# Layer A's first pass: the key and value products of a unit's two tiles in one PSUM bank ahead of both query products

## The chip, the cores and the metric

The kernel runs as one program on 1 core of one Trainium2 chip. The metric is the device time of one execution in microseconds (us), taken as the median of several runs. The core has five engines that run side by side and meet only at semaphores: PE (TensorE, matrix products, with PEld for its weight loads), ACT (ScalarE), DVE (VectorE), POOL (GpSimd) and SP (SyncE, which here only issues DMA transfers). PE writes its results to PSUM, eight banks of 128 partitions by 512 fp32 numbers; ACT and DVE read them from there.

## The reference

An inference step of a streaming encoder with two attention layers, over a prompt of 2048 tokens and a sample of 64 tokens with cached keys and values. Cut to what matters here:

```
def project(x, norm_g, w_in, q_g, k_g, n_heads, n_kv):
    h = rms_norm(x, norm_g)
    p = h @ w_in                          # (tokens, 1024) @ (1024, width)
    q, k, v, gate = jnp.split(p, ...)
    q = rms_norm(q per head, q_g)
    k = rms_norm(k per head, k_g)
    return q, k, v, gate

def gated_attention_layer(...):
    qp, kp, vp, gp = project(x_p, ...)
    op = prompt_band_attention(qp, kp, vp, past_chunks, bias_fn, sinks)
    y_p = x_p + (op * silu(gp)) @ w_out
    ...                                   # the same for the sample, with its cache
```

Layer A (the first) has 16 query heads of 64 and 2 key and value heads, a window of the own and two past chunks of 64 frames, a bias by relative position and a sink per head. Layer B has 16 key and value heads and a window of the own and eight past chunks. Everything is fp32 outside; inside, each product is made of three: high part by high part, high by low and low by high.

## The kernel before

**Tiles and units.** Tokens are worked in tiles of 128. Two tiles make a unit of 256 tokens (`units`, u = 0 to 7); the 64 sample tokens are a ninth unit (u == NU) with a single tile. The list `order` puts the sample in front of the last unit: 0, 1, 2, 3, 4, 5, 6, sample, 7.

**Passes.** Layer A goes over all units four times, `qd` = 0 to 3. Each pass projects 256 columns of queries and 256 of gates for four heads: a *query product* of 512 columns by 8 blocks of the model dimension by 3 matmuls, 24 matmuls of 512 columns (in `project`, L796, L797, L798; the sample's are L791 and L792, 16 of them). The first pass, `qd` = 0, also projects the 128 key and 128 value columns: a *key/value product* of 24 matmuls of 256 columns. Later passes reuse keys and values.

**PSUM.** Tag "pj" has two banks for the products, "o" one for attention outputs and small sums, "tp" one for transposes, and a pool "pa" with tag "sa" has four score banks. A buffer is given to a product when PE comes to its first matmul, from those that are free by the planner's own forecast of the times; the work on PE keeps the order in which the code emits it, and the other engines' instructions are ordered by the planner.

**Who empties a "pj" bank.** A key/value product is read by one ACT copy (`evacuate`, L819). A query product is read by ACT twice (`evacuate_a`: squares L835, gates L836) and last by DVE, which scales the queries by their norms (`norm_ps`, L890) after a sum on DVE (L883) and two steps on POOL (L886, L887). `in_banks(1)`, called before each new "pj" bank, emits the norms of all banks but the newest.

**The order around the change.** `layer_a` has a list of items, one per tile and pass. `Filler` is the stream of projection matmuls; `gen` of a unit yields after each block. `pipeline` walks the items: step i emits the scores of item i, then lets the filler run to 0.3 of the step, emits the transposes of probabilities of item i-1 (`values`), runs the filler to 0.6, emits the key transposes of item i+2 (`keys`, first pass only), runs to 0.8, emits the query and gate transposes (`turned`), runs to 0.95, emits the products with the values of item i-1 (`outputs`, L1452), and runs the filler to the end of the step. The end is the `mark` of item i+3, the point of the filler at which that item's products are finished.

In the first pass `gen` emits, for a unit's tiles 0 and 1: key/value product of 0, query product of 0, key/value product of 1, query product of 1, each in a "pj" bank of its own. Only the unit that comes last in `order` (u = 7, `heads_up`) emits both key/value products first, in two banks. Unit 0 has an order of its own (`first`) that the change does not touch. In unit 1 the scale of the values (`value_scales`, L290 to L297) is set with a small matmul into the "tp" bank, the token scales are made after tile 0's key/value product (`token_scales`), and rows of later units are loaded and squared (`row_scales`, L772) after each tile's.

Of the kernel before, what the change touches and what calls it, by code (L numbers as in the profile page):

```python
# [24 lines left out]
NU = SEQ // UT  # L25
# [33 lines left out]
def hybrid_encoder_kernel(  # L59
# [47 lines left out]
    def psum(tag, cols, bufs, pool=None):  # L107
        uid[0] += 1
        return (pool or pp).tile([P, cols], F32, tag=tag, name=f"{tag}_{uid[0]}", bufs=bufs)

    scores_pool = [None]
    psum_a = psum_b = lambda tag, cols, bufs: psum(tag, cols, bufs, scores_pool[0])
# [23 lines left out]
    held = {}  # L136
# [65 lines left out]
    def tp_bank():  # L202
        run_all("scales")
        return psum("tp", 512, 1)
# [85 lines left out]
        everywhere(9, row[:, 56:59])  # L290

    def value_scales():
        ps = tp_bank()
        nc.tensor.matmul(
            ps[:, 0:2], ones[0:1, 0:1].to_broadcast([1, P]), row[:, 44:46], start=True, stop=True
        )
        nc.vector.tensor_copy(sva, ps[:, 0:2])  # L297
# [427 lines left out]
    def token_scales(unit, x, ps):  # L725
        for q, q2 in zip(x.items, x.squares):
            bg.run(q)
            bg.run(q2)
        part = x.sum[0]
        _, T, tiles = unit  # L730
        sums_to_scales(0, tiles[0][0], [part[:, i * P : (i + 1) * P] for i in range(len(tiles))], ps)
# [49 lines left out]
    def project(tile_, xc, w, C, res, ps=None):  # L781
        tt, t0, n = tile_
        if ps is None:
            in_banks(1)
            ps = psum("pj", 512, 2)
            held["pj"].append([])
        for k in range(KC):
            wh, wl = weights_of(w, k)
            xh, xl = xc.parts[k // 2]
            if xl is None:  # L790
                nc.tensor.matmul(ps[:, :C], xh[:, k % 2, :], wh, start=k == 0, stop=False)  # L791
                nc.tensor.matmul(ps[:, :C], xh[:, k % 2, :], wl, start=False, stop=k == KC - 1)  # L792
                cost = 2 * C / 2400
            else:
                xh, xl = (a[:, k % 2, t0 : t0 + n] for a in (xh, xl))
                nc.tensor.matmul(ps[:n, :C], xh, wh, start=k == 0, stop=False)  # L796
                nc.tensor.matmul(ps[:n, :C], xh, wl, start=False, stop=False)  # L797
                nc.tensor.matmul(ps[:n, :C], xl, wh, start=False, stop=k == KC - 1)  # L798
                cost = 3 * C / 2400
            if k < KC - 1:  # L800
                yield cost
        res.append(ps)
        return cost
# [98 lines left out]
    def in_banks(n):  # L902
        while len(held["pj"]) > n:
            for it in held["pj"].pop(0):
                bg.run(it)
# [219 lines left out]
    def layer_a():  # L1125
        items = []
# [3 lines left out]
        def add_unit(qd, place, unit):  # L1130
            u, T, tiles = unit
            mine = []
            for tl in tiles:
                it = Item()
                it.qd, it.unit, it.tile, it.ready, it.todo = qd, unit, tl, False, []
                mine.append(it)
            items.extend(mine)

# [22 lines left out]
            def take_kv(it, ps):  # L1161
                tt, t0, n = it.tile
                last = u == NU
                it.kv = pr = evacuate(0, tt, n, ps, 256, 0)
                kn, v = pr[:n, 0:128], pr[:n, 128:256]
                if last:
                    split_v(n, v, VS[:, 1])
                else:
                    held["v"].append((VT[:, tt], v.rearrange("p (h d) -> p h d", d=HD)))
                if u == 1 and it is mine[0]:  # L1170
                    value_scales()
                while u and held["v"]:
                    vt, vv = held["v"].pop(0)
                    split_to(vt[:, :, 0:HD], vt[:, :, HD:P], vv, sva[:, 0:1])
                it.knorm = head_norm(n, kn, False)
                if last:
                    it.knorm.append(store_kv(0, slice(0, n), kn, v, ka_s[64:128, :], va_s[64:128, :]))
                elif tt == NT - 1:
                    it.knorm.append(store_kv(0, slice(0, n), kn, v, ka_p, va_p))
# [45 lines left out]

            def gen():
                xc = st.x.pop((qd, u))
                heads_up = qd == 0 and unit is order[-1]
                if heads_up:
                    for it in mine:  # L1230
                        out = []
                        c = yield from project(it.tile, xc, st.wkv, 256, out)
                        take_kv(it, out[0])
                        yield c
                for it in mine:
                    if qd == 0 and not heads_up:
                        out = []
                        c = yield from project(it.tile, xc, st.wkv, 256, out)
                        if u == 1 and it is mine[0]:
                            token_scales(unit, xc, psum("o", 512, 1))  # L1240
                        take_kv(it, out[0])
                        if u == 1:
                            row_scales(order[it.tile[0]])
                        yield c
                    out = []
                    c = yield from project(it.tile, xc, st.w[qd], 512, out)
                    take_qg(it, out[0])
                    if place:
                        spread_step()
                    if it is mine[-1]:  # L1250
                        if qd == 2 and place == 0:
                            bias_vectors_b()
                            keep(1)
                            held["heads"] += [(1, h) for h in range(16)]
                    yield c

            for it in mine:
                filler.total += 8 * (2 if it.tile[2] < P else 3) * (512 if qd else 768) / 2400
                it.mark = filler.total
            if qd == 0 and u == 0:  # L1260
                mine[0].mark = filler.total
            if qd == 0 and unit is order[-1]:
                mine[0].mark += 8 * 3 * 256 / 2400
            filler.add(prefetch, weights if place == 0 else None, first if qd == 0 and u == 0 else gen, 3 * (qd > 1))

        for qd in range(4):
# [1 line left out]
                add_unit(qd, place, unit)  # L1268

        def keys(it):  # L1270
            for q in it.knorm:
                bg.run(q)
            tt, t0, n = it.tile
            tp = psum_a("sa", 512, 4)[:, :n]
            transpose(tp, it.kv[:n, 0:128])
            gk = (kf, ksc)[it.unit[0] == NU][:, 0:1]
            if it.unit[0] == NU:
                kd = [a[:, CA : CA + TS] for a in (KSA, KSB)]
            else:
                kd = [a[:, tt * P : (tt + 1) * P] for a in (KA, KB)]  # L1280
            for kk, rows in zip(kd, halves):
                nc.scalar.activation(kk[0:64], tp[rows], AF.Identity, scale=gk[rows])
            for kk, rows in zip(kd, halves):
                nc.vector.scalar_tensor_tensor(
                    kk[64:128], tp[rows], gk[rows], wide(kk[0:64]),
                    op0=ALU.mult, op1=ALU.subtract,
                )
# [220 lines left out]
        def pipeline():  # L1508
            N = len(items)
            for i in range(-3, N + 1):  # L1510
                c0 = filler.done
                end = c0 + 5.2
                if i + 3 < N:
                    end = max(items[i + 3].mark, c0 + AVG_A)
                filler.attending = i >= 0
                scales_ahead(i)
                if 0 <= i < N:
                    scores(items[i])
                    if i == N - 1:
                        held["scored"] = True  # L1520
                    bg.share(AL, AP_, 3)
                filler.to(c0 + 0.3 * (end - c0))
                if 0 <= i < N:
                    turn_a(items[i])
                if 0 <= i - 1:
                    values(items[i - 1])
                    bg.share(AL, AP_, 3)
                if 0 <= i + 2 < N and items[i + 2].qd == 0:
                    filler.to(c0 + 0.6 * (end - c0))
                    keys(items[i + 2])  # L1530
                filler.to(c0 + 0.8 * (end - c0))
                turned(items[i + 2] if 0 <= i + 2 < N else None, items[i - 1] if 0 <= i - 1 else None)
                filler.to(c0 + 0.95 * (end - c0))
                if 0 <= i - 1:
                    outputs(items[i - 1])
                filler.to(end)
                assert i + 3 >= N or items[i + 3].ready
# [1083 lines left out]
```

## Time and profile before

| what | before |
|---|---|
| median of 3 runs | 2065.02 us (2062.98 to 2066.77) |
| the profiled execution's own time | 2071.44 us |
| its span, first to last instruction | 2069.7 us |
| mean granted TensorE clock | 0.992 |
| ACT busy | 1438.7 us (70%) |
| DVE busy | 1440.7 us (70%) |
| POOL busy | 1134.8 us (55%) |

A profile is one execution. Busy time is the time in which an engine has an instruction running. A line such as L796 is the line of the kernel that made the instruction, and "out<-in" names the tiles that it writes and reads. "idle before <-X" says which instruction ended the engine's idle time. The first pass of layer A, with the start-up, fills about the first 220 us of the span; all later passes and layer B have no key/value product of this kind.

### The profile page before, as it was taken

The numbers are of one execution on the slowest core, as the hardware profiler recorded it, in microseconds if no ns is written. First come the engines' busy times: TensorE is split into PE (matmuls) and PEld (weight loads), VectorE is DVE, ScalarE is ACT, GpSimd is POOL, SyncE is SP. The second block draws the span as 40 slices with busy tenths as digits, with TensorE's granted clock in tenths as the row PEclk, the third lists the DMA queues.
The fourth block names the chain that finished last, engine by engine and source line by source line (L and its number), as shares of the span: only waits on it lengthen the run. The fifth ranks groups of instructions, "written<-read, shape, count | busy, mean of one in ns | idle before, by whom it ended". The sixth has DMA issues, their size and how long they took to land.

```text
span 2069.7 us, 40501 instructions
## 1 busy us (share of the span) xinstructions
PE 1975.7 (95%) x12723; PEld 1382.1 (67%) x12723; DVE 1440.7 (70%) x4163; ACT 1438.7 (70%) x3560; POOL 1134.8 (55%) x1529
## 2 busy tenths in 40 slices
PE   7899999999999999989999999999999999999999
PEld 6777777777877888545555555555555555557788
DVE  7666877877778433677667676676767767677673
ACT  6887888777789443377677787786877778687330
POOL 5665565544446323477556575665656656565540
PEclk9999999999999999999999999999999999999999
DMA  8878887998776555698989788897997978698753
GB/s 264 260 210 233 230 215 207 238 243 243 206 187 192 168 177 162 229 235 219 237 177 237 177 201 220 168 253 162 212 211 182 215 167 187 151 189 205 189 158 106
DMA packets 593816, 420.20 MB, mean 203 GB/s; under 512 B 403696, under 2 KB 522880, under 8 KB 593568
## 3 DMA queue, kind: packets, MB, share of 16 engines
q1 hardware_dynamic: 593600, 417.60, 79.9%
q8 instruction: 101, 1.65, 0.3%
q14 instruction: 115, 0.94, 0.1%
HBM read 248.68 MB, written 73.43 MB: 156 GB/s over the span
## 4 chain that ended last, share of the span: by engine, by line
PE 58%; DVE 12%; DMA 10%; ACT 8%; issue 6%; POOL 5%; SPq 1%; POOLq 0%; ACTq 0%; DVEq 0%
PE pj L796 11%; PE pj L798 10%; PE pj L797 10%; PE o L1908 4%; DMA pt<-values 3%; PE sb L1744 2%; PE pj L2164 2%; PE sb L1745 2%; PE pj L2166 2%; PE pj L2165 2%; PE tp L1054 2%; PE pj L2413 2%; PE pj L2417 2%; PE pj L2416 2%; DVE p L1748 1%
## 5 line engine op out<-in xcount | busy, mean ns | idle before, releaser
L796 PE MATMUL pj<-wh,xx 128*128 128x512 f16 (+2 forms) x1648 | 642.9, 390 | 19.8 <-ACT pa L819 9.1
L798 PE MATMUL pj<-wh,xx 128*128 128x512 f16 (+2 forms) x1648 | 624.6, 379 | 0.0
L1801 POOL TENSOR_TENSOR values<-p,values 128x640 f16<-128x640 f32 (+4 forms) x256 | 328.2, 1282 | 206.9 <-ACT values L1800 202.7
L797 PE MATMUL pj<-wh,xx 128*128 128x512 f16 x1024 | 389.9, 381 | 1.3 <-DVE wh L582 1.3
L1760 ACT ACTIVATE p<-p,nm 128x640 f32<-128x640 f32 (+5 forms) x264 | 199.6, 756 | 181.4 <-DVE nm L1753 148.7
L1748 DVE CUSTOM_DVE_ANT_0 p<-sb,BT 128x640 f32<-128x640 f32 (+5 forms) x272 | 196.4, 722 | 148.1 <-PE sb L1745 120.9
L797 PE MATMUL pj<-wl,xx 128*128 128x512 f32 (+1 forms) x624 | 234.8, 376 | 2.3 <-DVE wl L582 2.3
L887 POOL TENSOR_TENSOR f<-f,mhalf 128x4 f32<-128x4 f32 x182 | 188.0, 1033 | 11.7
L798 PEld LDWEIGHTS <-xx 128*128 128x128 f16 x1024 | 100.6, 98 | 123.6 <-issue 3.8
L1561 POOL TENSOR_TENSOR o<-gt,o 128x256 f32<-128x256 f32 (+1 forms) x132 | 106.4, 806 | 139.5 <-ACT p L1391 63.9
L1800 ACT CAST values<-p 128x640 f16<-128x640 f32 (+4 forms) x256 | 168.2, 657 | 12.7 <-DMA pt<-values 6.5
L1391 ACT ACTIVATE p<-p,nm 128x257 f32<-128x257 f32 (+2 forms) x272 | 134.3, 496 | 59.3 <-DVE nm L1380 26.6
L797 PEld LDWEIGHTS <-xx 128*128 128x128 f16 x1024 | 100.6, 98 | 84.2 <-issue 4.9
L796 PEld LDWEIGHTS <-xx 128*128 128x128 f16 x1024 | 100.6, 98 | 82.0 <-issue 1.9
L1908 PEld LDWEIGHTS <-values 128*128 128x128 f16 x1344 | 123.8, 98 | 41.2 <-issue 2.8
L1908 PE MATMUL o<-pt,values 128*128 128x256 f16 (+1 forms) x1344 | 144.7, 256 | 3.6 <-DMA pt<-values 3.6
L796 PEld LDWEIGHTS pj<-wh,xx 128*128 128x128 f32 x624 | 118.6, 190 | 40.3 <-ACT pa L819 11.0
L798 PEld LDWEIGHTS pj<-wh,xx 128*128 128x128 f32 x624 | 118.4, 190 | 23.1
L886 POOL TENSOR_TENSOR f<-f,small 128x4 f32<-128x4 f32 x182 | 38.5, 211 | 172.5 <-DVE f L883 152.7
L797 PEld LDWEIGHTS pj<-wl,xx 128*128 128x128 f32 x624 | 119.1, 191 | 17.6 <-DVE wl L582 3.2
L1556 ACT COPY o<-o 64x256 f32<-64x256 f32 (+1 forms) x264 | 96.1, 364 | 37.8 <-PE o L1908 27.3
L678 POOL TENSOR_TENSOR xx<-xraw,xx 128x512 fp32r<-128x512 f32 (+3 forms) x80 | 97.4, 1233 | 44.3 <-ACT xx L677 44.0
(389 smaller groups left out, 5157.7 us busy)
## 6 DMA issues: line engine op xcount, KB each, us to landing
xx<-xsb SPq DMA_DIRECT2D x112, 512.0 KB, 4.3
xx<-xsa SPq DMA_DIRECT2D x88, 512.0 KB, 5.0
xsa<-xx SPq DMA_DIRECT2D x32, 512.0 KB, 4.2
wl<-in_w_in_b_dram SPq DMA_DIRECT2D x64, 256.0 KB, 4.8
wraw<-in_w_in_b_dram SPq DMA_DIRECT2D x56, 256.0 KB, 3.6
xraw<-in_x_dram SPq DMA_DIRECT2D x40, 256.0 KB, 4.4
xraw<-oga SPq DMA_DIRECT2D x32, 264.0 KB, 3.2
xraw<-ogb SPq DMA_DIRECT2D x32, 264.0 KB, 3.5
```

Of the source, the lines that this page charges most:

```text
L678: nc.gpsimd.tensor_tensor(lo, rv, wide(hi), op=ALU.subtract)
L796: nc.tensor.matmul(ps[:n, :C], xh, wh, start=k == 0, stop=False)
L797: nc.tensor.matmul(ps[:n, :C], xh, wl, start=False, stop=False)
L798: nc.tensor.matmul(ps[:n, :C], xl, wh, start=False, stop=k == KC - 1)
L887: nc.gpsimd.tensor_tensor(fv, fv, mhalf[:n, :H], op=ALU.pow)
L1391: ex = nc.scalar.activation(pv[:n, h % 2, : nk + 1], pv[:n, h % 2, : nk + 1], AF.Exp, scale=-1.0, bias=nm[:n, h : h + 1], accum_out=sm[:n, ...
L1561: nc.gpsimd.tensor_tensor(o1v, gtv, o1v, op=ALU.mult)
L1748: mi = nc.vector.tensor_tensor_reduce(out=p[r, :nk], in0=S[r, o : o + nk], in1=b, op0=ALU.add, op1=ALU.min, scale=1.0, scalar=3e38, accum_ ...
L1760: ex = nc.scalar.activation(p[:n, :nk], p[:n, :nk], AF.Exp, scale=-1.0, bias=it.nm[:n, c : c + 1], accum_out=it.sm[:n, c : c + 1],)
L1800: hi = nc.scalar.copy(two[:, :, 0, :], pv)
L1801: lo = nc.gpsimd.tensor_tensor(two[:, :, 1, :], pv, two[:, :, 0, :], op=ALU.subtract)
L1908: nc.tensor.matmul(it.O[:, h * T + q0 : h * T + q1_], held["VH"][:, kt, h], x, start=kt == kb and not low, stop=kt == tb and low == 1,)
```

## The change

The unit's two key/value products are emitted one after the other into the two halves of a single "pj" bank, and then both query products; so a unit takes three "pj" banks in place of four, and all two-tile units of the first pass but unit 0 have the order that only u = 7 had. The copies out of the bank (`take_kv`) are emitted after both products. The sample's key/value product goes to a score bank ("sa"). In unit 1 the value scale's small matmul goes to a score bank too, and the token scales, both tiles' copies and both row loads are emitted after the second product. The marks of both tiles of a unit are moved back by one key/value product (only the first tile's in the last unit of `order`), since tile 0's query product now ends that much later and the following step would otherwise be short. The key transposes of a unit's second tile (`pair`) move from 0.6 of their own step to 0.95 of the step before, behind `turned` and in front of `outputs`; `known` marks items whose keys are done.

```
     def value_scales():
-        ps = tp_bank()
+        ps = psum_a("sa", 512, 4)
...
                 it.qd, it.unit, it.tile, it.ready, it.todo = qd, unit, tl, False, []
+                it.known, it.pair = False, None
...
             def gen():
                 xc = st.x.pop((qd, u))
-                heads_up = qd == 0 and unit is order[-1]
-                if heads_up:
-                    for it in mine:
-                        out = []
-                        c = yield from project(it.tile, xc, st.wkv, 256, out)
-                        take_kv(it, out[0])
+                if qd == 0:
+                    if u == NU:
+                        ps = psum_a("sa", 512, 4)
+                    else:
+                        in_banks(1)
+                        ps = psum("pj", 512, 2)
+                        held["pj"].append([])
+                    kvs = [ps[:, 256 * i : 256 * i + 256] for i in range(len(mine))]
+                for it, kv in zip(mine, kvs) if qd == 0 else ():
+                    c = yield from project(it.tile, xc, st.wkv, 256, [], kv)
+                    if it is not mine[-1]:
                         yield c
-                for it in mine:
-                    if qd == 0 and not heads_up:
-                        out = []
-                        c = yield from project(it.tile, xc, st.wkv, 256, out)
-                        if u == 1 and it is mine[0]:
-                            token_scales(unit, xc, psum("o", 512, 1))
-                        take_kv(it, out[0])
+                if qd == 0:
+                    if u == 1:
+                        token_scales(unit, xc, psum("o", 512, 1))
+                    for it, kv in zip(mine, kvs):
+                        take_kv(it, kv)
                         if u == 1:
                             row_scales(order[it.tile[0]])
-                        yield c
+                    yield c
+                for it in mine:
                     out = []
                     c = yield from project(it.tile, xc, st.w[qd], 512, out)
                     take_qg(it, out[0])
...
+            if qd == 0 and len(mine) == 2:
+                mine[0].pair = mine[1]
             if qd == 0 and u == 0:
                 mine[0].mark = filler.total
-            if qd == 0 and unit is order[-1]:
+            elif qd == 0 and len(mine) == 2:
                 mine[0].mark += 8 * 3 * 256 / 2400
+                if unit is not order[-1]:
+                    mine[1].mark += 8 * 3 * 256 / 2400
...
         def keys(it):
+            it.known = True
...
-                if 0 <= i + 2 < N and items[i + 2].qd == 0:
+                key = items[i + 2] if 0 <= i + 2 < N and items[i + 2].qd == 0 else None
+                if key is not None and not key.known:
                     filler.to(c0 + 0.6 * (end - c0))
-                    keys(items[i + 2])
+                    keys(key)
                 filler.to(c0 + 0.8 * (end - c0))
                 turned(items[i + 2] if 0 <= i + 2 < N else None, items[i - 1] if 0 <= i - 1 else None)
                 filler.to(c0 + 0.95 * (end - c0))
+                if key is not None and key.pair is not None:
+                    keys(key.pair)
                 if 0 <= i - 1:
                     outputs(items[i - 1])
```

## The prediction

> **What bounds the kernel now.** The page's busy shares come first, then the busy time of each engine in two stretches, the first pass with the start-up and all the rest:
>
> ```profile
> span 2069.7 us, 40501 instructions
> PE 1975.7 (95%) x12723; PEld 1382.1 (67%) x12723; DVE 1440.7 (70%) x4163; ACT 1438.7 (70%) x3560; POOL 1134.8 (55%) x1529
> 0.00:210.00 210.00, 180.90 (x1097) 151.72 (x1098) 146.85 (x491) 161.02 (x425) 125.39 (x182) 0.98 0.83 241
> 210.00:2070.00 1860.00, 1794.84 (x11628) 1230.41 (x11626) 1293.82 (x3673) 1277.66 (x3136) 1009.36 (x1348) 0.99 0.80 199
> ```
>
> PE sets the end: 95% busy, nobody else over 70%. But in the first 210 us it idles for 29 us (14%), in the other 1860 for 65 (3.5%). (After the width come busy us of PE, PEld, DVE, ACT, POOL; granted clock; DMA share; GB/s.) The change touches only that first stretch. The view of waits for PE up to 330 us says what it waits for there:
>
> ```profile
> PE pj L796 <- ACT pa L819: 9.1, 4, 3.1
> PE pj L796 <- DVE pa L890: 6.4, 5, 1.8
> PE pj L791 <- DVE pa L890: 1.3, 1, 1.3
> PE tp L294 <- DVE scrow L194: 0.9, 1, 0.9
> PE tp L1054 <- DVE sva L297: 0.7, 1, 0.7
> ```
>
> Total, count, longest. Ten waits of 16.8 us stand before products into "pj": four for the ACT copy that empties a key/value product, six for DVE's last read of a query product. The last two rows, 1.6 us, are unit 1's value scale. Now the stretches by unit, cut where each first key/value product starts: units 2 to 6, the sample, unit 7, and one stretch of the second pass:
>
> ```profile
> 56.77:84.10 27.33, 23.61 (x144) 19.70 (x141) 21.29 (x65) 23.74 (x67) 18.36 (x30) 0.94 0.91 269
> 84.10:110.96 26.86, 22.87 (x150) 19.35 (x147) 15.00 (x58) 20.51 (x56) 15.55 (x23) 1.00 0.75 215
> 110.96:135.86 24.90, 22.61 (x149) 19.20 (x147) 16.68 (x57) 20.99 (x58) 16.96 (x24) 1.00 0.92 244
> 135.86:159.39 23.53, 22.67 (x149) 19.23 (x147) 16.06 (x56) 18.73 (x55) 13.82 (x23) 1.00 0.74 207
> 159.39:186.93 27.54, 24.29 (x149) 20.41 (x147) 14.68 (x58) 19.72 (x55) 13.53 (x22) 0.94 0.73 189
> 186.93:196.81 9.88, 8.56 (x60) 7.21 (x58) 8.85 (x27) 8.63 (x25) 7.87 (x12) 1.00 0.98 333
> 196.81:219.41 22.60, 22.60 (x149) 19.02 (x147) 20.24 (x69) 19.07 (x49) 12.06 (x17) 1.00 0.87 234
> 245.62:262.80 17.18, 16.61 (x100) 13.41 (x97) 13.05 (x44) 15.25 (x42) 12.85 (x21) 1.00 0.81 224
> ```
>
> Unit 7 is the pattern: it already makes both key/value products first and takes 22.60 us with PE busy for all of it. Units 2 to 6 do the same products in 27.33, 26.86, 24.90, 23.53 and 27.54 us, 130.2 in all. Units 2 and 6 also show a granted clock of 0.94: 6% of 27.4 us is 1.6 us of lost clock in each. The timeline of PE shows where:
>
> ```profile
> 74.62 0.50 PE L796 MATMUL pj<-wh,xx 128*128 128x512 f32 x1 [1.95 <-ACT pa L819]
> 75.20 0.39 PE L798 MATMUL pj<-wh,xx 128*128 128x512 f32 x1
> ...
> 76.11 0.63 PE L798 MATMUL pj<-wh,xx 128*128 128x512 f32 x1
> ```
>
> After a wait of 1.95 us the products slow from 0.39 to 0.63 us for a while. The Trainium skill, in "TensorE: Matmul & The Clock Gate", section "What's actually happening", has the array fall to half clock after an idle window of about 3.4 us; here the wait before the slow stretch is shorter than that. By that rule these waits would not be what costs the clock, unit 6 would keep its 1.6 us, and the sum below would come out 1.6 us smaller.
>
> **What the change removes.** Which bank a query product waits for is seen at two places (PE, then ACT and DVE):
>
> ```profile
> 84.10 0.36 PE L796 MATMUL pj<-wh,xx 128*128 128x256 f32 x1
> ...
> 86.89 0.28 PE L798 MATMUL pj<-wh,xx 128*128 128x256 f32 x1
> ...
> 90.43 0.51 PE L796 MATMUL pj<-wh,xx 128*128 128x512 f32 x1 [2.82 <-ACT pa L819]
> 91.01 0.40 PE L798 MATMUL pj<-wh,xx 128*128 128x512 f32 x1
> ...
> 93.11 0.39 PE L798 MATMUL pj<-wh,xx 128*128 128x512 f32 x1
> ...
> 96.44 0.40 PE L798 MATMUL pj<-wh,xx 128*128 128x512 f32 x1
> ...
> 98.35 0.36 PE L796 MATMUL pj<-wh,xx 128*128 128x256 f32 x1
> ...
> 103.04 0.51 PE L796 MATMUL pj<-wh,xx 128*128 128x512 f32 x1 [1.17 <-ACT pa L819]
> ```
>
> ```profile
> 102.51 0.47 ACT L819 ACTIVATE pa<-pj,rms 128x256 f32<-128x256 f32 x1
> ```
>
> ```profile
> 104.01 0.47 DVE L890 SCALAR_TENSOR_TENSOR pa<-pj,rms,f 128x256 f32<-128x256 f32 x1
> ```
>
> The query product at 103.04 starts when the ACT copy ends (102.98) and before DVE has read the older query product (104.48): it took the bank that its own key/value product just filled. In the other cases it waits for the older query product. Either way only one short product lies between: 24 matmuls of 256 columns from 84.10 to 86.89, 2.9 us, against 24 of 512 columns at (93.11 - 91.01)/9 = 0.233 us, 5.6 us. How long DVE's last read takes after a query product, at best and at worst of the twelve in the pass:
>
> ```profile
> 157.48 0.40 PE L798 MATMUL pj<-wh,xx 128*128 128x512 f32 x1
> ...
> 168.91 0.40 PE L798 MATMUL pj<-wh,xx 128*128 128x512 f32 x1
> ```
>
> ```profile
> 162.31 0.48 DVE L890 SCALAR_TENSOR_TENSOR pa<-pj,rms,f 128x256 f32<-128x256 f32 x1
> ...
> 178.13 0.47 DVE L890 SCALAR_TENSOR_TENSOR pa<-pj,rms,f 128x256 f32<-128x256 f32 x1
> ```
>
> 4.9 us (157.88 to 162.79) and 9.3 us (169.31 to 178.60). A tile's attention on PE is (22.60 - 2 x 2.9 - 2 x 5.6)/2 = 2.8 us, of which 1.7 is outputs and scores (from 96.44 plus one step of 0.23 to 98.35). After the change the first query product must find the bank of the previous unit's second one: two short products and 2.8 us, 8.6 us of cover. The shared bank must find the first query product's bank: 5.6 us and all but the turns and outputs of a tile, about 7.1. The second query product needs two ACT copies that have 5.6 us and more, against waits of 1.2 to 3.1 now. So most waits go; what is late next is ACT.
>
> **How far it shrinks.** ACT has 18.73 to 23.74 us of work per unit. In the second-pass row it is busy for 15.25 of 17.18 us, 89%, and PE still idles only 0.57; in unit 7 it is 84% and PE idles not at all. I hold units 3 and 4 to that 89%: 20.51/0.89 = 23.0 and 20.99/0.89 = 23.6. Units 5 and 6 need less and get unit 7's 22.6. Unit 2's 23.74 lies between 23.74 (ACT full) and 26.7 (89%); its transfers are 0.91 x 27.33 = 24.9 us; I take 25.0. Sum 116.8, **13.4 us less**. The bounds are 17.2 (all at 22.6) and, by the rival below, 8.3.
>
> Unit 1: its value-scale matmul comes 2.9 us later and uses a score bank, so both its waits (1.6 us) go; one wait for L890 (up to 1.8) goes if cover holds. Bounds 0 and 3.4; I take **2.5**. The sample's 1.3 goes, its key/value product being out of "pj": **1.3**.
>
> **What it adds.** No matmul, copy or transfer is added; all are moved. Tile 0's copy now waits for tile 1's matmuls, 2.9 us more, then ACT does two L819 of 0.47 in a row in front of exponentials and square reads; nothing on PE asks for tile 0's keys before 0.6 of a step after its query product. Every wait of PE for a bank holds all of PE's queue: turns, outputs, scores. `turned` asks for a first query product's norms 6.1 filler units after it (a short product counts 2.56 units and takes 2.9 us, so 6.9 us), about 8.4 us with scores and transposes between, against the 4.9 to 9.3: up to 0.9 in the worst case. Unit 1's eight row loads go to SP's queue together, before later loads of x; the sample holds a score bank, and two key transposes in one step take two. No wait for a score bank is in the view of waits, so nothing below; above, one such wait is at most the longest of a bank now, 3.1. I take **1.0** for all, nearest to the many cases without a wait, between 0 and 4. The rest of the program is the same code; its instructions can fall differently, which I put at 0 plus or minus 2, the scatter of the three times before.
>
> Sum: 13.4 + 2.5 + 1.3 - 1.0 = 16.2 us. It comes from an execution of 2071.44 us, 6.4 above the median; waits are what I subtract, so I take them from the median: 2065.0 - 16.2 = **2048.8, say 2049**. All waits and lost clock gone is 16.8 + 1.6 + 3.2 = 21.6: 2043.4.
>
> **Rivals.** *ACT sets the pace.* ACT's idle time is itself made of waits that do not shrink with PE's. If each unit keeps the 3.6 us that unit 2 has (27.33 - 23.74), units 2 to 6 come to 27.3, 24.1, 24.6, 22.6 (no less) and 23.3, 121.9 in all: 8.3 us, with half of unit 1 and sample (1.9) less 1.0 about 9: **2056**. For it: ACT over 90% in three units. Against: unit 7 and the second pass.
>
> *Nothing is gained.* Transfers fill 0.83 of the first 210 us; if they set the units' lengths, or the delayed ACT work comes back as waits in the second pass, 2061 to 2069, **2065**. Against: 0.98 and 333 GB/s in the sample's stretch, with PE's idle time there a bank wait.
>
> *Slower: the planner gives the first query product the shared bank itself.* Then PE waits in every unit for two copies, not one: the four such waits now average 9.1/4 = 2.3, so 2.8 with a second copy of 0.47, and at worst 3.6; two of the four are in the units with lost clock, so 0.8 to 1.6 each. Seven units, unit 7 now among them, give 25 to 36 us against 21.6 removed: 3 to 15 slower, **2074** in the middle. It decides from 21.6/7 = 3.1 us per unit. The Trainium skill bears on it: "PSUM — Partial Sum Buffer", "Summary: rules for kernel authors", says to read a bank other than the one being written, and the shared bank is read only after all its writes. For it: the choice at 90.43 and 103.04. Against: the other bank has 8.6 us to come free, and only the worst of twelve exceeds that.
>
> **How the numbers follow.** Forecast (2042 to 2053) 0.62; ACT (2053 to 2061) 0.20; nothing gained 0.11; slower 0.07. The two first make faster by over 0.2% (4.1 us, about what a measurement of this kernel can tell from no change): 0.82; same 0.11; slower 0.07. The range 2042 to 2060 leaves out the last two and a little of the second.
>
> **What would show it.** Right: no wait of a 512-column product for L819, at most a few for L890, units 2 to 6 at 22.6 to 25 us, clock near 1.00 there, no L294 wait. Wrong: waits for L819 before each first query product (the slower rival); new PE waits for ACT or DVE at turns and outputs (ACT's); stretches as long as now with transfers near 1 (nothing gained); or a difference that arises after 220 us.

## The result and the profile after

| what | before | after |
|---|---|---|
| median | 2064.74 us of 6 runs (2062.98 to 2067.17) | 2054.72 us of 6 runs (2053.43 to 2056.33) |
| ratio, 95% interval | | 0.995, 0.9938 to 0.9962 |
| profiled execution, and its span | 2071.44 us, 2069.7 | 2055.78 us, 2052.9 |

The change gains 10.0 us where 16.2 were forecast. The products with the values, L1452 before, are L1462 now; DVE's reads of the scores, L1380, are L1390; its steps on nm, L1386, are L1396; the work on x and the norms of the queries keep their lines. First the page, then busy time by stretches cut as in the prediction: units 1 to 6, the sample, unit 7 up to the first product of the second pass. After the width come PE, PEld, DVE, ACT, POOL, granted clock, DMA share and GB/s.

```profile
span 2052.9 us, 40512 instructions
PE 1970.2 (96%) x12723; PEld 1381.7 (67%) x12723; DVE 1433.6 (70%) x4163; ACT 1433.9 (70%) x3560; POOL 1128.3 (55%) x1529
```

```profile
33.61:52.99 19.38, 19.38 (x119) 16.99 (x118) 14.94 (x66) 14.97 (x42) 10.46 (x15) 0.97 0.93 310
52.99:74.72 21.73, 20.75 (x132) 17.81 (x131) 16.86 (x60) 18.96 (x56) 13.09 (x19) 1.00 0.87 265
74.72:103.98 29.26, 24.76 (x146) 21.07 (x147) 17.70 (x62) 24.18 (x69) 19.08 (x32) 0.88 0.94 254
103.98:126.94 22.96, 22.41 (x148) 19.38 (x147) 16.60 (x56) 19.84 (x57) 16.27 (x24) 1.00 0.92 267
126.94:149.76 22.82, 22.45 (x149) 19.37 (x147) 15.83 (x56) 18.22 (x53) 15.00 (x24) 1.00 0.80 209
149.76:174.02 24.26, 22.60 (x149) 19.51 (x147) 14.94 (x56) 17.16 (x52) 11.37 (x21) 1.00 0.78 190
174.02:183.71 9.69, 8.61 (x60) 7.36 (x58) 6.56 (x16) 8.87 (x25) 8.07 (x9) 1.00 1.08 270
183.71:209.82 26.11, 25.02 (x169) 21.16 (x167) 23.60 (x86) 24.04 (x64) 14.54 (x23) 1.00 0.92 288
```

Units 2 to 6 sum to 121.0 us (130.2 before, 116.8 forecast). Units 2, 4 and 5 come out near the forecast or below it and unit 6 takes 1.7 us more than forecast; unit 3 takes 29.26 us, more than before, with a granted clock of 0.88. PE's waits up to 330 us (total, count, longest):

```profile
PE pj L796 <- DVE nm L1396: 6.0, 3, 4.5
...
PE o L1462 <- DVE pl L1020: 2.6, 3, 1.1
PE o L1462 <- ACT ph L1019: 1.2, 1, 1.2
PE sa L1054 <- DVE KB L1294: 1.1, 1, 1.1
PE tp L1054 <- DVE pa L890: 0.8, 1, 0.8
...
PE pj L796 <- DVE pa L890: 0.4, 1, 0.4
```

No wait for L819, L294 or L297 is left. New are small waits at outputs and transposes, and 6.0 us in front of products; 4.5 of these stand at one place, as PE's timeline shows:

```profile
82.84 0.60 PE L1054 MATMUL sa<-ident,p 128*128 128x128 f32 x4
87.94 0.76 PE L796 MATMUL pj<-wh,xx 128*128 128x512 f32 x1 [4.50 <-DVE nm L1396]
88.50 0.63 PE L797 MATMUL pj<-wl,xx 128*128 128x512 f32 x1
...
92.34 0.58 PE L797 MATMUL pj<-wl,xx 128*128 128x512 f32 x1
92.76 0.39 PE L798 MATMUL pj<-wh,xx 128*128 128x512 f32 x1
```

This is unit 3's first query product. After the wait ten steps take 92.76 - 88.50 = 4.26 us; at 0.23 each they would take 2.3, so half clock costs some 2 us more. The bank that it needs holds unit 2's second query product, which ended at 73.64. What became of that product on the other engines, in the timeline of all of them:

```profile
79.12 0.47 ACT L835 ACTIVATE sq<-pj,rms 128x256 f32<-128x256 f32 x1
...
79.62 0.42 DVE L883 TENSOR_REDUCE f<-sq 128x4 f32<-128x256 f32 x1 [1.55 <-ACT sq L835]
...
80.37 1.29 POOL L678 TENSOR_TENSOR xx<-xraw,xx 128x512 fp32r<-128x512 f32 x1
...
82.04 0.20 POOL L886 TENSOR_TENSOR f<-f,small 128x4 f32<-128x4 f32 x1
82.19 1.28 POOL L678 TENSOR_TENSOR xx<-xraw,xx 128x512 fp32r<-128x512 f32 x1
83.56 1.00 POOL L887 TENSOR_TENSOR f<-f,mhalf 128x4 f32<-128x4 f32 x1
...
86.43 0.84 DVE L1573 TENSOR_TENSOR o<-o,o 64x256 f32<-64x256 f32 x2
87.31 0.48 DVE L890 SCALAR_TENSOR_TENSOR pa<-pj,rms,f 128x256 f32<-128x256 f32 x1
```

ACT squares it 5.5 us after its end; the sum is ready at 80.04, but POOL is making low parts of x (L678) and takes the sum's step at 82.04 and the root at 83.56, with another L678 between; DVE then has keys, scores and outputs ahead of L890. From the product's end to DVE's last read are 87.79 - 73.64 = 14.1 us, against the 8.6 us of cover and the 9.3 us that the prediction took as the worst. The same product in the kernel before, on all engines:

```profile
82.18 0.40 PE L798 MATMUL pj<-wh,xx 128*128 128x512 f32 x1
...
83.09 0.47 ACT L835 ACTIVATE sq<-pj,rms 128x256 f32<-128x256 f32 x1
...
90.45 0.47 DVE L890 SCALAR_TENSOR_TENSOR pa<-pj,rms,f 128x256 f32<-128x256 f32 x1
```

There ACT's square came 0.5 us after the product's end (82.58) and the last read ended 8.3 us after it. From the square to the end of the last read it took 7.8 us then and 8.7 now. So 5.0 of the 5.8 us by which the latency grew stand in front of ACT's square, where ACT is busy with other work, and 0.8 behind it; the low parts of x stood in that chain on POOL before as well. (The view of waits names L1396 because it came last on DVE in front of PE's start; the bank was released by L890 at 87.79, PE started at 87.94.)

Both programs run the same code behind the first pass. The table sets the start of the second pass's first product, the time from there to PE's last matmul, and PE's idle time from 30 us to that start (summed over its instructions) beside the ratio of each run, for this result and all the experiments:

| run | ratio to before, 95% interval | second pass starts | from there to the end | PE idle in the first pass |
|---|---|---|---|---|
| before | 1 | 219.4 | 1846.6 | 20.0 |
| before_again | | 221.0 | 1839.5 | 20.9 |
| after | 0.995, 0.9938 to 0.9962 | 209.8 | 1839.4 | 10.2 |
| after_again | 0.9956, 0.994 to 0.9971 | 209.0 | 1838.6 | 9.6 |
| two_banks | 1.0051, 1.0033 to 1.0069 | 226.7 | 1838.1 | 25.0 |
| bare | 0.9965, 0.9951 to 0.998 | 212.2 | 1834.2 | 16.4 |
| scale_bank | 1.0006, 0.9988 to 1.0025 | 218.3 | 1839.4 | 16.9 |
| sample_pj | 0.9991, 0.9977 to 1.0006 | 217.1 | 1845.5 | 15.5 |
| act_copy | 0.9957, 0.9943 to 0.9972 | 210.6 | 1843.5 | 10.3 |
| rows_later | 0.9971, 0.9957 to 0.9985 | 213.5 | 1841.2 | 12.7 |
| norm_now | 0.9963, 0.9948 to 0.9977 | 209.2 | 1840.8 | 11.6 |
| before_norm_now | 1.0006, 0.9993 to 1.0018 | 218.8 | 1838.5 | 19.8 |
| split_dve | 0.9947, 0.9932 to 0.9963 | 207.3 | 1839.3 | 8.9 |
| split_two | 0.9943, 0.9928 to 0.9959 | 211.0 | 1843.6 | 13.0 |

The first pass ends 9.6 us earlier, which is the whole gain. The two profiled executions of the result stand 15.7 us apart, because the profiled execution of before holds some 7 us of its own behind the first pass. That part differs between executions (1834.2 to 1846.6 here), so a run's pass and its ratio need not agree to the microsecond.

### The profile page after: what moved, and what is told of

It is laid out like the page before. It is cut to its first block, busy times and chain, and to the rows that moved or that the text cites. A ratio compares the mean times of both kernels' runs of the same rounds, so it can differ in the third digit from the quotient of the medians.

```text
span 2052.9 us, 40512 instructions
## 1 busy us (share of the span) xinstructions
PE 1970.2 (96%) x12723; PEld 1381.7 (67%) x12723; DVE 1433.6 (70%) x4163; ACT 1433.9 (70%) x3560; POOL 1128.3 (55%) x1529
## 4 chain that ended last, share of the span: by engine, by line
PE 61%; DVE 13%; DMA 9%; ACT 8%; issue 5%; POOL 3%; SPq 1%; ACTq 0%; POOLq 0%; DVEq 0%
PE pj L796 11%; PE pj L797 11%; PE pj L798 11%; PE o L1921 4%; PE pj L2177 2%; PE pj L2179 2%; PE pj L2178 2%; PE sb L1757 2%; PE sb L1758 2%; DMA pt<-values 2%; PE tp L1054 2%; DVE p L1761 2%; PE pj L2426 1%; PE pj L2430 1%; PE pj L2429 1%
## 5 line engine op out<-in xcount | busy, mean ns | idle before, releaser
L887 POOL TENSOR_TENSOR f<-f,mhalf 128x4 f32<-128x4 f32 x182 | 187.7, 1031 | 11.8
L886 POOL TENSOR_TENSOR f<-f,small 128x4 f32<-128x4 f32 x182 | 38.0, 209 | 163.8 <-DVE f L883 143.9
L678 POOL TENSOR_TENSOR xx<-xraw,xx 128x512 fp32r<-128x512 f32 (+3 forms) x80 | 96.3, 1217 | 44.4 <-ACT xx L677 44.3
```

The source lines that it names most:

```text
L678: nc.gpsimd.tensor_tensor(lo, rv, wide(hi), op=ALU.subtract)
L887: nc.gpsimd.tensor_tensor(fv, fv, mhalf[:n, :H], op=ALU.pow)
```

## The experiments

### The same kernels again

The kernel before and the changed one, each without an edit, on two different chips.

> The kernel before, profiled once more. Theory A: the change is worth what the first pass shows, about 10 us, and the other 6 us by which the two profiled spans differ (2069.7 and 2052.9) were waits and lost clock that only that one execution of the kernel before had in layer B, between 900 and 1050 us and near 1930. Then this profile's first pass again takes about 185 us from unit 1's first key/value product to unit 7's last query product, its waits for L819 and L890 again sum to 14 to 18 us, but its span lies nearer 2063. Theory B: the first pass itself varies between executions; then the pass takes 180 us or less here and the waits in it are fewer. Theory C: layer B's waits come from where the first pass ends, and are there again: span 2068 to 2071 with the same waits at 900 to 1050 us.

Its time was 2065.84 us; the first pass ends at 221.0 as in the first profile, the rest is 7 us shorter. So the excess over the median in the profile of before did not belong to what the change removes.

> The changed kernel again, beside the three below. Theory A: ratio 0.995 as before; its first pass again has one long wait ahead of unit 3's first query product (4.5 us in the first profile), since it comes from the planner's order on ACT, POOL and DVE, which is fixed. Theory G: that wait is a matter of one execution, and is under 1.5 us here.

Unit 3 waits again, 4.02 us at 87.30. So it is not a matter of one execution. That it comes from the fixed order in which the engines' work is listed fits this, but is argued.

### Which part carries the gain

**Two banks**: both key/value products first, but each in a product bank of its own.

```
-                    kvs = [ps[:, 256 * i : 256 * i + 256] for i in range(len(mine))]
-                for it, kv in zip(mine, kvs) if qd == 0 else ():
-                    c = yield from project(it.tile, xc, st.wkv, 256, [], kv)
+                for it in mine if qd == 0 else ():
+                    if u != NU:
...
+                    kvs.append(ps[:, 0:256])
+                    c = yield from project(it.tile, xc, st.wkv, 256, [], kvs[-1])
```

> The changed kernel, with each key/value product in a bank of its own again (both still ahead of the query products). Theory A: it is the cover of a bank that counts. The second key/value product then needs the bank of the query product before it with only one short product, 2.9 us, and a little attention between, against 4.9 to 9.3 us that the bank takes to come free; so PE waits before second key/value products for L890, 2 to 5 us per unit in units 2 to 6, and most of the gain is lost: 2060 to 2070 us. Theory D: it is the order alone (copies have a whole query product of time); then the time stays at 2053 to 2057 us, as unit 7 had it in the kernel before.

The waits of PE up to 330 us in this run:

```profile
PE pj L796 <- ACT pa L819: 15.7, 4, 4.8
PE pj L796 <- DVE pa L890: 6.6, 1, 6.6
```

Slower than before. Units 2 to 5 wait 3.3 to 6.6 us before their second key/value product; the longest wait for L819, 4.8 us, stands in front of unit 1's first query product, when both banks hold key/value products. In unit 2 the second product takes the bank of the last query product of the unit before, with one short product of 2.9 us between, and waits for L890. In units 3 to 5 it takes the bank that the first key/value product has just filled: PE starts 0.05 us after ACT's copy ends (94.79, 122.11 and 150.14), in unit 3 before DVE's last read of the older query product is done (95.55). The order alone is worth less than nothing; without the shared bank there is no gain. (Unit 7 of the kernel before has just this order and no wait, but there the sample's products stand in front of it.)

**Bare**: the changed kernel without the shift of the second tiles' marks and without the move of their key transposes.

```
-            if qd == 0 and len(mine) == 2:
-                mine[0].pair = mine[1]
...
-                if unit is not order[-1]:
-                    mine[1].mark += 8 * 3 * 256 / 2400
```

> The changed kernel without the later mark of a unit's second tile and without moving its key transposes: steps of the pass are 10.2 and 5.1 filler units long in turn instead of 7.7 each. Theory A (bank cover) says that most of the gain stays, 2053 to 2060 us, with some waits more where a short step holds a whole tile's attention. Theory E: the even steps are the gain; then 2062 us or more.

```profile
PE tp L1054 <- DVE pa L890: 5.3, 4, 2.0
PE tp L1054 <- DVE nm L1392: 4.0, 3, 2.7
PE o L1458 <- DVE pl L1020: 2.9, 5, 1.0
```

PE's waits move to the turns, 9.3 us in seven, but the pass still ends 7.2 us earlier than before. So most of the gain stands without the even steps. The 2.4 to 3.1 us by which the pass ends later than in the two profiles of the changed kernel are too little for the ratios, whose intervals overlap. This kernel still has the sample's score bank, and the next edit but one shows how much hangs on that.

**The value scale**: the kernel before with that one product in a score bank.

```
     def value_scales():
-        ps = tp_bank()
+        ps = psum_a("sa", 512, 4)
```

> The kernel before with one edit: the value scale's small matmul goes to a score bank. Theory A: only the wait of the query transposes in unit 1 goes (0.7 us, for L297), the wait of L294 stays (0.9 us), so within 1 us of the kernel before, 2063 to 2066 us. Theory F: unit 1 sets the pace of what follows and this edit carries a third of the gain or more: 2061 us or less.

Ratio 1.0006: nothing that can be measured. The two waits for it are gone, and the pass ends 1.1 to 2.7 us earlier than in the two profiles of before, too little to show in the times.

**The sample's bank**: the changed kernel, with the sample's key/value product in a product bank.

```
-                    if u == NU:
-                        ps = psum_a("sa", 512, 4)
-                    else:
-                        in_banks(1)
-                        ps = psum("pj", 512, 2)
-                        held["pj"].append([])
+                    in_banks(1)
+                    ps = psum("pj", 512, 2)
+                    held["pj"].append([])
```

> The changed kernel with the sample's key/value product in a product bank in place of a score bank. Theory A: the sample's query product then needs the bank of unit 6's second query product, with only 16 short matmuls and a tile's attention between; a wait for L890 of 0.5 to 2 us comes back there, the rest stays: 0 to 2 us slower than after_again. Else: no difference, since the wait at the sample was lost among others.

```profile
PE pj L796 <- DVE nm L1393: 4.1, 1, 4.1
PE pj L791 <- DVE pa L890: 4.1, 1, 4.1
...
PE o L1459 <- ACT ph L1019: 2.5, 1, 2.5
```

2065.27 us against 2056.99 for the changed kernel on the same chip: 8.3 us, where my term was 1.3. The ratio's interval holds 1: without the sample's score bank the rest of the change can't be told from the kernel before, so the gain needs the shared bank and the sample's score bank together. The sample's query product then has to find a bank with only one short product between, and waits 4.1 us for L890, and PE's idle time in the pass rises from 9.6 to 15.5. Of the 8.1 us by which the pass ends later, 2.3 are not idle time of PE. The sample's own stretch, from its key/value product to unit 7's first, takes 14.40 us for 8.41, so 6.0 of the 8.1 us arise there.

### What holds unit 3 up

**Copied by ACT**: in the changed kernel unit 2's second query product is copied out by ACT (`evacuate`) and normed later, so its bank does not wait for POOL and DVE.

```
-                if n == P and (qd or unit is not order[0]):
+                if n == P and (qd or unit is not order[0]) and (qd or tt != 5):
```

> The changed kernel, where the second tile of unit 2 has its queries and gates copied out of the bank by ACT and normed in SBUF, so that its bank no longer waits for DVE's sums, POOL's two steps and DVE's scaling (79.62 to 87.79 in the first profile), but for ACT alone (79.96). If the long wait at unit 3 is that chain, it goes, and with it the slow stretch behind it: 4 to 7 us less than after_again in the first pass. If ACT itself is the pace of units 2 and 3, the wait comes back as others (unit 3's copies, exponentials), and the pass is within 2 us of after_again's.

```profile
111.40 0.47 PE L796 MATMUL pj<-wh,xx 128*128 128x512 f32 x1 [3.62 <-DVE nm L1396]
```

Unit 3's wait is gone, and the next unit waits 3.62 us instead, with half clock behind it; the time is the changed kernel's.

**Rows later**: unit 3's row loads and squares one unit later, meant to take them out of ACT's stretch in question.

```
-                        if u == 1:
-                            row_scales(order[it.tile[0]])
+                        if u == 1 and it is mine[0] or u == 2 and it is mine[1]:
+                            row_scales(order[2 if u == 1 else 3])
```

> The changed kernel, with the rows of unit 3 loaded and squared one unit later, so that unit 1's end issues four row loads in place of eight. Theory H: the bunch of row squares on ACT (L772, eight of 0.63 us between 60 and 78 us) is why unit 2's second query product was first read 5.5 us after its end; then the wait at unit 3 falls to 2 us or less and the time by 2 to 5 us. Theory I: POOL's splits of x hold the norm steps anyway; the wait stays at 3 us or more.

```profile
91.05 0.79 PE L796 MATMUL pj<-wh,xx 128*128 128x512 f32 x1 [4.57 <-ACT pa L819]
```

Unit 3 waits as long, and the pass ends 3.7 us later than in the changed kernel's profile. In this program the planner gave unit 3's first query product the shared bank itself, so PE waits for both copies (the second ended at 91.00); the other bank's L890 ended at 90.14, 13.5 us after its product. But the edit did not clear the stretch: the eight row squares that run from 53.0 to 77.6 us in the changed kernel, four of them behind 60, run from 62.3 to 78.6 here, and ACT's square of the product still came 4.5 us late. So this run says nothing on the row squares as a cause.

**Norm at once**: the norm steps of the pass's query products (both of a unit) are handed to the planner as soon as the product is.

```
                     it.pr, it.gate, norm = evacuate_a(tt, ps, 512, 256)
+                    if qd == 0:
+                        for q in norm:
+                            bg.run(q)
```

> The changed kernel, but the norm's sums and scaling of each second query product are put on the engines' lists at once, ahead of the x splits and row squares of the next unit, instead of when the planner finds them due. Theory late release (the bank of unit 2's second query product comes free 14 us after the product because its norm steps are listed behind x splits on POOL and row squares on ACT): unit 3's wait of 4.5 us goes or stays under 1 us, its half clock with it, and the first pass ends 4 to 7 us earlier: ratio 0.992 to 0.994 against the kernel before. Theory ACT's pace (the engines are full in this stretch and the order only moves the wait): as much waiting comes back before other products, turns or outputs, and the time stays within 2 us of the changed kernel's: ratio 0.995 to 0.996. Theory overshoot: x splits that come later hold the next tiles' turns or products up, and it is 3 us or more slower than the changed kernel: ratio above 0.997.

POOL's timeline in this run, at the same place:

```profile
79.17 1.29 POOL L678 TENSOR_TENSOR xx<-xraw,xx 128x512 fp32r<-128x512 f32 x1
...
80.83 0.20 POOL L886 TENSOR_TENSOR f<-f,small 128x4 f32<-128x4 f32 x1
80.99 1.28 POOL L678 TENSOR_TENSOR xx<-xraw,xx 128x512 fp32r<-128x512 f32 x1
...
82.35 1.01 POOL L887 TENSOR_TENSOR f<-f,mhalf 128x4 f32<-128x4 f32 x1
```

The order on POOL is the same as without the edit: L678, L886, L678, L887. Unit 3 waits 4.08 us. It seems that the planner puts these steps where its own clock has them due, however early they are handed over. So this run says nothing for or against either theory.

> The kernel before with the same edit alone: norm sums and scaling of each second query product listed at once, the order of the products as before. Theory cover (the product between is too short, 2.9 us, whatever the norm's place in the lists): the waits for L819 stay at 9 us in four, those for L890 shrink by half at most, and it gains 0 to 4 us: ratio 0.998 to 1.000. Theory late release alone (the waits of the kernel before came from late norms as well, and an early norm does what the change does): waits for L890 gone, 6 to 10 us gained: ratio 0.995 to 0.997.

```profile
PE pj L796 <- ACT pa L819: 9.5, 3, 4.5
...
PE pj L796 <- DVE pa L890: 5.7, 5, 1.8
```

The same edit in the kernel before: the waits stay, and so does the time. Since the edit hardly reaches the engines' order, this speaks only weakly for the theory that the cover was too short.

**POOL relieved**: the changed kernel with the low parts of unit 4's x, which POOL makes in that stretch, on DVE.

```
-                    nc.gpsimd.tensor_tensor(lo, rv, wide(hi), op=ALU.subtract)
+                    low = nc.vector if dt == F32R and o == 4 * UT else nc.gpsimd
+                    low.tensor_tensor(lo, rv, wide(hi), op=ALU.subtract)
```

> The changed kernel, but the low parts of unit 4's x, which are made while unit 2's last norm is under way, are taken on DVE instead of POOL. Theory POOL (the norm's sum L886 started 2.4 us late behind POOL's x splits of 1.29 us each): unit 3's wait of 4.5 us falls to 1.5 us or less, and 2 to 5 us are gained on the changed kernel: ratio 0.993 to 0.995. Theory whole chain (ACT's square and DVE's scaling are as late by themselves): the wait stays at 3 us or more, or comes back elsewhere, and the time stays within 2 us of the changed kernel's: ratio 0.995 to 0.996.

The same chain in the timeline of this run (lines behind L678 are one higher):

```profile
77.98 0.47 ACT L836 ACTIVATE sq<-pj,rms 128x256 f32<-128x256 f32 x1
...
78.71 0.41 DVE L884 TENSOR_REDUCE f<-sq 128x4 f32<-128x256 f32 x1
...
80.18 0.20 POOL L887 TENSOR_TENSOR f<-f,small 128x4 f32<-128x4 f32 x1
...
80.92 1.20 POOL L888 TENSOR_TENSOR f<-f,mhalf 128x4 f32<-128x4 f32 x1
...
82.92 0.48 DVE L891 SCALAR_TENSOR_TENSOR pa<-pj,rms,f 128x256 f32<-128x256 f32 x1
...
83.56 0.47 PE L797 MATMUL pj<-wh,xx 128*128 128x512 f32 x1 [0.88 <-DVE pa L891]
...
110.06 0.47 PE L797 MATMUL pj<-wh,xx 128*128 128x512 f32 x1 [2.81 <-DVE pa L891]
```

From ACT's square to the end of DVE's read are 5.4 us instead of 8.7: POOL's x work was 3.3 us of it, and unit 3's wait falls from 4.5 to 0.9, without half clock. So it is shown that this work held up most of that wait; the 5.2 us between the product's end and ACT's square are still there, and no run took them away. And a wait of 2.81 us with half clock stands at unit 4 now, where ACT's square comes 4.5 us after the product, L888 again late behind x work on POOL, and L891 behind keys, outputs and scores on DVE. The pass ends 1.7 to 2.5 us earlier than in the two profiles of the changed kernel; the ratio, 0.9947, can't be told from 0.995.

**POOL relieved twice**: unit 5's low parts too (`o in (4 * UT, 5 * UT)`).

> The changed kernel with the low parts of unit 4's and of unit 5's x on DVE instead of POOL. With unit 4's alone, unit 3's wait fell from 4.5 to 0.9 us, but unit 4's first query product then waited 2.8 us, and there POOL's x splits for unit 5 again stood ahead of the norm steps L886 and L887. Theory POOL: unit 4's wait falls to 1 us or less as well, unit 3's stays under 1.5, and the first pass ends 2 to 4 us before the run with unit 4's alone: ratio 0.992 to 0.994 against the kernel before. Theory pace of ACT and DVE (what POOL gives up is now late there): a wait of 2 us or more comes back at unit 4, 5 or 6 or at the turns and outputs, and the pass ends within 1 us of the run with unit 4's alone: ratio 0.994 to 0.996.

```profile
PE pj L797 <- DVE nm L1397: 3.1, 2, 2.1
PE o L1463 <- ACT ph L1020: 3.1, 2, 2.7
```

Unit 4's wait is gone too, but 2.07 us came at unit 3's first product (76.24) and 2.73 us at outputs (166.15), and in the profiled execution, the slowest of its six, the pass ends 3.6 us later than in the run before. The theory of ACT's and DVE's pace fits better, though it had the pass within 1 us. The ratio, 0.9943, is the lowest of all, and its interval holds the changed kernel's: no version was shown to be better.

## Why the prediction came out as it did

- **What bounds the kernel, and where the gain is from: right.** Waits for L819, L294 and L297 are all gone, the gain lies in the first pass, and the rest takes 1839.4 us, as in three of the four profiles of the old order (1838.5 to 1839.5). Taking the subtraction from the median and not from the profiled execution was right as well.
- **Units 2 to 6: mechanism right, size off by 4.2 us** (121.0 for 116.8). Unit 2 came out 3.3 us better than the 25.0 taken, unit 4 0.6 better, unit 5 0.2 worse, unit 6 1.7 worse, with new waits of 1.21 and 0.46 us for outputs. Unit 3 was 6.3 us worse than its 23.0. The step that failed is "the other bank has 8.6 us to come free, and only the worst of twelve exceeds that". The twelve latencies were read from the kernel before, where the five second query products of units 2 to 6 took 8.3, 5.9, 5.3, 4.9 and 5.2 us to their L890. In the changed kernel they took 14.1, 8.8, 8.6, 3.6 and 8.5: the cover is missed by 4.5 us of PE and 2 us of half clock at unit 3, and by 0.55 and 0.37 us at units 4 and 5. The latencies of the first query products grew by 0.5 us at most; one of them, at 8.3 us, outlasted the 7.1 us that the shared bank was given, for a wait of 0.97. (All are read off PE's and DVE's timelines.) And 4.5 + 2 is about the 6.2 us by which the sum was too large, while the errors of all other terms cancel to about half a microsecond, which is luck.
- **Why the worst latency grew.** In unit 2 the growth is nearly all ACT's: its second product ends 8.9 us earlier than before, and ACT's square comes only 4.0 us earlier. That PE's own waits had given ACT time to catch up fits this, but no run tests it. Nor was the worst a fixed number: in the second profile of the kernel before the same product took 10.2 us.
- **Unit 1 and what was added.** Unit 1 came out 4.5 us shorter for 2.5, but it holds 119 matmul records for 127, and unit 7's stretch 169 for 149, with 3.5 us more: the shifted marks moved work from units 1 and 2 to the last stretch (unit 2 holds 132 records for 144). Of the 3.5 us, 2.4 are this work and 1.1 a wait; of unit 1's 4.5 us, 3.5 are idle time of PE and 1.0 is work that left. Part of unit 2's 3.3 us is such work too. New waits, put at 1.0 with all other added costs, were 1.08 (key transposes in the sample), 1.67 (unit 6's outputs) and 1.09 (the first outputs behind unit 7, for L1020): 3.8 us. They are the waits for turns and outputs that the prediction named as the sign of ACT's rival.
- **The sample.** Its wait of 1.3 went, 1.08 came: 9.88 to 9.69 us. The term was small for another reason too: it was read as the wait seen in the old order, while in the new order a product bank cost the whole kernel 8.3, some 6 of it in the sample's stretch.
- **The sum.** Against the forecast the stretches from unit 1 to the second pass differ by -4.2 (units 2 to 6), +2.0 (unit 1), -1.1 (sample) and -2.5 (unit 7's 3.5 in place of the 1.0 added): 16.2 - 5.8 = 10.4, and the two profiles show 186.5 - 176.2 = 10.3 between the same points. PE's idle time in these stretches falls by 8.7 us, and its busy time by 1.6.
- **ACT sets the pace** gave 2056. The measured 2054.7 lies in the interval given to this rival (2053 to 2061) and outside the forecast's own (2042 to 2053). Its mechanism does not hold unit by unit: units 4 and 5 take 22.96 and 22.82 us with ACT at 86% and 80%, where that rival had 24.6 and 22.6. It comes nearest in the one stretch with 24.18 us of ACT and 19.08 us of POOL, where ACT's square is 5.5 us late and POOL's work adds 3.3 us. In the runs that eased that wait, one came back elsewhere each time, which fits the pace of these engines together as the next limit, without showing it. The "ACT over 90% in three units" that the prediction counts for this rival is not in its rows: 23.74, 20.51 and 20.99 us are 87, 76 and 84% of the units' lengths before, and 95, 89 and 89% of those forecast.
- **Nothing gained** fell: the pass ends 9.6 us earlier, with DMA shares of 0.78 to 1.08 in its stretches, and the part behind it takes as long as in three of the four profiles of the old order. **Slower** fell: no first query product waits for L819, and each wait that is left at a product ends 0.15 us after an L890 (74.57, 87.79, 112.92 and 135.67), so after a query product's last read and not after a copy. The kernel before gave some query products the bank of their own key/value product. Its mechanism is real all the same: with the rows later it came up in one unit, and cost a wait of 4.57 us there, over the 2.8 to 3.6 at which I had priced it.
- **Clock.** Units 2 and 6 were forecast to win back their 1.6 us each, and both show 1.00 now; so the other reading, by which unit 6 would keep its 1.6, did not come true. Unit 3 lost some 2 instead.

## What to carry to other kernels

A latency that is read while the bottleneck engine itself is waiting can be too short for the program in which it no longer waits (8.3 us became 14.1 here); when waits of the bottleneck are removed, allow for the other engines coming to that work late, most of all where a short step has long independent steps listed in front of it. Two products that are read by the same cheap copy can share a bank, and the gain lies in how long the *other* bank then has to come free: the order alone, without the shared bank, made this kernel slower, and one further product in a product bank, the sample's, took back nearly all of the gain. Compare stretches and not whole profiles, since one execution can hold several us of its own.

## What was unexpected of the hardware

- PE fell to half clock after waits of 4.50 us (changed kernel), 4.57 (rows later), 3.62 (copied by ACT) and 2.81 us (POOL relieved), and after 1.95 and 3.14 us in the kernel before, but not after 2.82 us there, at 90.43. So a wait's length alone does not tell whether half clock follows. Nor does the clock fall when the wait ends: in the changed kernel the granted clock is 1.00 for the first 2.46 us of the wait (83.44 to 85.90) and 0.50 from there to 92.73, and in the kernel before it fell at 75.64, 1.0 us after PE had started again. The Trainium skill, "TensorE: Matmul & The Clock Gate", section "What's actually happening", has an idle window of about 3.4 us that runs freely; the waits of 3.62 us and more are longer than that, those of 1.95, 2.81 and 3.14 us came to half clock below it, and here the measurement decides.
- The same subtraction of 128x512 elements (low parts of x) takes 1.29 us on POOL and 0.69 us on DVE, so a short norm step listed behind one waits longer on POOL.
